# A hybrid encoder step on one core: 32 sample tokens moved from the dense expert pass to gathered rows

## The chip, the cores and the metric

The kernel runs on one core of one Trainium2 chip. The metric is the device time of one execution in microseconds (us). Three runs of the kernel before are at hand, and one profiled execution.

## What is computed

Two layers of a streaming encoder are applied to 512 prompt tokens and 32 sample tokens (544 tokens of width 1024). Each layer has a token mixer (attention, state-space scan, pooling) and then the PEER channel mixer, which takes most of the time and which the change is about. The reference, cut to that:

```python
def peer(x, w_q, sub_keys, u_tab, v_tab):          # 16384 experts, u_tab and v_tab of 16384 x 1024
    q = (xb @ w_q).reshape(blk, PEER_HEADS, 2, D_HALF)
    s = jnp.einsum('nhpd,hpkd->nhpk', q, sub_keys)
    sv, si = lax.top_k(s, PEER_TOPK)               # 16 of 128 keys, twice, for each of 8 heads
    cand = (sv[:, :, 0, :, None] + sv[:, :, 1, None, :]).reshape(blk, PEER_HEADS, 256)
    cv, ci = lax.top_k(cand, PEER_TOPK)
    ...
    eid = i1 * N_KEYS + i2                         # 128 expert slots for each token
    g = jax.nn.softmax(cv, axis=-1)
    act = jax.nn.gelu(jnp.einsum('nd,nhkd->nhk', xb, u_tab[eid]), approximate=False)
    return jnp.einsum('nhk,nhkd->nd', (g * act).astype(xb.dtype), v_tab[eid])
```

## The kernel before

The tokens lie in five tiles: tile 0 to 3 of 128 tokens, tile 4 of the 32 sample tokens. A token's 128 slots can be served in two ways, and the kernel uses both.

- **Gathered rows.** For tile 0, `gather` (lines 260 to 274) fetches with one indirect DMA on POOL's queue, for each of the 128 partitions, the row of u and v of that token's expert in one slot (1 MB). VectorE (DVE) makes the dot product with u (`junk`, line 268), ScalarE (ACT) its gelu (line 271), DVE the gate product (line 272) and the sum with v (`accg`, line 274). There are 128 such gathers in a layer, with three `uv` buffers. `gstep` paces them: each step of the dense loop has a weight (`WD1`, `WD2`), and gathers are issued in proportion.
- **Dense pass.** For the other 416 tokens (`ND`) all 16384 experts are computed, in 128 blocks of 128. `upass` (line 137) makes the 24 matmuls of a block with u (three products of high and low float32r parts over 8 pieces), each of 128x128 weights and 416 columns. `load_split` (line 125) loads 512 KB, copies the high part on ACT (line 132) and subtracts for the low part on DVE (line 133); it has three `raw` buffers. The activations are multiplied with a gate table G (expert by token), split again, and multiplied with v, 24 matmuls a block again (line 215).

A layer's PEER goes through these stages:

1. `topk` (line 285): queries, scores, and the two top-16 selections on DVE for each tile, and from them the slot tables (expert indices and gates, transposed).
2. `gbuild` (line 395) makes G in 52 steps of 8 tokens: four DVE products of 128x1024 f16 (lines 405 to 410: two comparisons, the gate's high part, the gate's low part), 16 small matmuls, two ACT evictions (line 419).
3. The spill pass (lines 170 to 174): the u pass of the first `NSPILL` = 80 blocks, whose activations go to DRAM (`AC`).
4. The dense loop (lines 182 to 232): groups of four blocks; 20 groups read their activations back from `AC`, 12 compute them with `upass`; every group makes the v pass, and the gathers run beside it.

The order of instructions on each engine is set when the kernel is built, by a scheduler that goes by the priority of the program order and by which buffers it expects to be free. On the chip each engine keeps that order, so an instruction that waits holds up those behind it. The spill pass stands behind `topk` and `gbuild` in priority, and the scheduler fills in its blocks where it sees room.

## Time and profile before

| | |
|---|---|
| median of 3 runs | 3354.44 us (3349.73 to 3357.75) |
| the profiled execution | 3355.85 us, of which the span from the first to the last instruction is 3354.1 us |
| PE (matmul) busy | 3123.9 us, 93% of the span |
| DVE busy | 2665.7 us, 79% |
| ACT busy | 1245.7 us, 37% |
| POOL busy | 644.0 us, 19% |
| mean granted TensorE clock | 0.965 |
| DMA | 781.56 MB, mean 233 GB/s |

A matmul's bar in the profile is longer than the distance to the next one, since they overlap in the array; a rate is therefore read from runs of matmuls in the chain of waits (time over count). The same holds, less strongly, for DVE and ACT: the distance between the starts of two instructions that follow each other is what one costs. "DMA share" is the mean busy share of the core's 16 DMA engines. The two layers show the same stages, the second some 1630 us after the first.

### The profile page before, as it was taken

The numbers are of one execution on the slowest core, as the hardware profiler recorded it, in microseconds if no ns is written. First come the engines' busy times: TensorE is split into PE (matmuls) and PEld (weight loads), VectorE is DVE, ScalarE is ACT, GpSimd is POOL, SyncE is SP. The second block draws the span as 40 slices with busy tenths as digits, with TensorE's granted clock in tenths as the row PEclk, the third lists the DMA queues.
The fourth block names the chain that finished last, engine by engine and source line by source line (L and its number), as shares of the span: only waits on it lengthen the run. The fifth ranks groups of instructions, "written<-read, shape, count | busy, mean of one in ns | idle before, by whom it ended". The sixth has DMA issues, their size and how long they took to land.

```text
span 3354.1 us, 48383 instructions
## 1 busy us (share of the span) xinstructions
PE 3123.9 (93%) x17932; PEld 2960.0 (88%) x17932; DVE 2665.7 (79%) x5685; ACT 1245.7 (37%) x2215; POOL 644.0 (19%) x436
## 2 busy tenths in 40 slices
PE   5779967999999999999999998789999999999998
PEld 5667967999999999999988688689999999999998
DVE  7976599993398898888974638999627989899888
ACT  3243323453333333333344423245433333333333
POOL 4443011100021222222210410120001222222221
PEclk8889988999999999999999999899999999999999
DMA  3113223677599999999952132257847999999996
GB/s 119 52 33 115 85 87 115 250 269 245 174 344 334 326 338 350 343 330 340 344 174 67 51 117 90 98 172 278 294 162 263 345 337 346 327 342 343 338 337 248
DMA packets 328265, 781.56 MB, mean 233 GB/s; under 512 B 24318, under 2 KB 178142, under 8 KB 291676
## 3 DMA queue, kind: packets, MB, share of 16 engines
q1 hardware_dynamic: 291164, 510.01, 45.1%
q0 software_dynamic: 36864, 268.45, 20.6%
q8 instruction: 141, 2.31, 0.3%
q14 instruction: 96, 0.79, 0.1%
HBM read 677.65 MB, written 100.73 MB: 232 GB/s over the span
## 4 chain that ended last, share of the span: by engine, by line
PE 48%; issue 22%; DVE 20%; DMA 7%; ACT 2%; POOL 1%; SPq 0%; POOLq 0%; ACTq 0%; DVEq 0%
PE psa L145 12%; PE psb L215 12%; PE psc L215 6%; PE psa L215 6%; DMA raw<-in_peer_uv 4%; PE psa L1012 3%; DVE ul L133 2%; DVE wl L133 1%; DMA uv<-in_peer_uv,eid 1%; DMA act<-AC 1%; DVE trep L281 1%; DVE accg L274 1%; DVE junk L268 1%; DVE X L280 1%; DVE X L283 1%
## 5 line engine op out<-in xcount | busy, mean ns | idle before, releaser
L145 PE MATMUL psa<-hh,ul 128*128 128x416 f32 (+1 forms) x2304 | 807.9, 355 | 87.7 <-DVE ul L133 87.7
L145 PE MATMUL psa<-hh,uh 128*128 128x416 f32 (+1 forms) x2304 | 805.3, 353 | 8.5 <-ACT uh L132 8.4
L145 PE MATMUL psa<-hl,uh 128*128 128x416 f32 (+1 forms) x2304 | 798.9, 350 | 0.0
L265 POOL DMA_INDIRECT uv<-in_peer_uv,eid x256 | 376.5, 1471 | 1770.5 <-DVE accg L274 1673.5
L133 DVE TENSOR_TENSOR ul<-raw,uh 128x1024 fp32r<-128x1024 f32 x268 | 345.3, 1290 | 278.4 <-ACT uh L132 278.2
L145 PEld LDWEIGHTS psa<-hh,ul 128*128 128x128 f32 x2304 | 440.1, 192 | 102.8 <-DVE ul L133 98.4
L132 ACT ACTIVATE uh<-raw 128x1024 fp32r<-128x1024 f32 x272 | 287.5, 1058 | 599.8 <-PE psa L145 510.4
L145 PEld LDWEIGHTS psa<-hh,uh 128*128 128x128 f32 x2304 | 440.7, 193 | 17.5 <-ACT uh L132 12.2
L145 PEld LDWEIGHTS psa<-hl,uh 128*128 128x128 f32 x2304 | 440.3, 193 | 6.0
L132 ACT ACTIVATE wh<-raw 128x1024 fp32r<-128x1024 f32 (+1 forms) x303 | 314.9, 1047 | 229.4 <-DMA raw<-in_peer_uv 165.3
L133 DVE TENSOR_TENSOR wl<-raw,wh 128x1024 fp32r<-128x1024 f32 (+1 forms) x281 | 342.5, 1222 | 55.3 <-ACT wh L132 54.6
L215 PE MATMUL psb<-wh 128*128 128x416 f32 x1024 | 358.1, 353 | 7.2 <-ACT wh L132 7.2
L215 PE MATMUL psb<-wh,wl 128*128 128x416 f32 x1024 | 359.4, 352 | 3.2 <-DVE wl L133 3.1
L215 PE MATMUL psb<-wl,wh 128*128 128x416 f32 x1024 | 357.9, 350 | 0.0
L274 DVE SCALAR_TENSOR_TENSOR accg<-uv,gw,accg 128x1024 f32<-128x1024 f32 x256 | 327.9, 1281 | 3.0
L268 DVE SCALAR_TENSOR_TENSOR junk<-uv,xg 128x1024 f16<-128x1024 f32 x256 | 312.0, 1219 | 21.4 <-DMA uv<-in_peer_uv,eid 21.0
L271 ACT ACTIVATE gw<-gact 128x1 f32<-128x1 f32 x256 | 50.7, 199 | 468.0 <-DVE junk L268 466.8
L196 ACT ACTIVATE wh<-act 128x416 fp32r<-128x416 f32 x256 | 139.2, 549 | 228.0 <-DVE act L194 126.6
L215 PEld LDWEIGHTS psb<-wh 128*128 128x128 f32 x1024 | 192.6, 188 | 11.1 <-ACT wh L132 9.3
L215 PEld LDWEIGHTS psb<-wh,wl 128*128 128x128 f32 x1024 | 192.5, 188 | 7.6 <-DVE wl L133 5.3
L215 PEld LDWEIGHTS psb<-wl,wh 128*128 128x128 f32 x1024 | 192.9, 188 | 1.8
L215 PE MATMUL psc<-wh 128*128 128x416 f32 x512 | 180.1, 352 | 4.9 <-ACT wh L132 4.9
(548 smaller groups left out, 5722.6 us busy)
## 6 DMA issues: line engine op xcount, KB each, us to landing
raw<-in_peer_uT SPq DMA_DIRECT2D x256, 512.0 KB, 4.4
raw<-in_peer_uv SPq DMA_DIRECT2D x256, 512.0 KB, 7.1
G<-st SPq DMA_DIRECT2D x26, 2048.0 KB, 7.3
gt<-G SPq DMA_DIRECT2D x64, 832.0 KB, 11.1
AC<-act SPq DMA_DIRECT2D x160, 208.0 KB, 2.0
act<-AC SPq DMA_DIRECT2D x160, 208.0 KB, 8.8
raw<-in_w_out SPq DMA_DIRECT2D x16, 512.0 KB, 3.3
raw<-in_peer_wq SPq DMA_DIRECT2D x16, 512.0 KB, 3.3
```

Source lines behind the costliest of these rows:

```text
L132: nc.scalar.activation(hi, raw, AF.Copy)
L133: (eng or nc.vector).tensor_sub(lo, raw, hi)
L145: nc.tensor.matmul(pss[i][:, :c - a], w[:, k, :], x[:, k, a:c], start=(k == 0 and j == 0), stop=(k == 7 and j == 2))
L196: nc.scalar.activation(wh, a_, AF.Copy)
L215: nc.tensor.matmul(ps[:, :ND], w[:, d % 4 * 128:(d % 4 + 1) * 128], x, start=(first and q == 0 and j == 0), stop=(last and q == GB - 1 and ...
L265: nc.gpsimd.indirect_dma_start(out=uv, out_offset=None, in_=s.I['peer_uv'].rearrange('l e d -> (l e) d'), in_offset=bass.IndirectOffsetOnA ...
L268: nc.vector.scalar_tensor_tensor(junk, uv[:, 0:1024], 1.0, s.xg, op0=ALU.mult, op1=ALU.mult, accum_out=act[:, i:i + 1])
L271: nc.scalar.activation(w, act, AF.Gelu)
L274: nc.vector.scalar_tensor_tensor(s.accg, rows[i][:, 1024:2048], w[:, i:i + 1], s.accg, op0=ALU.mult, op1=ALU.add)
L280: nc.vector.max_index(idx[:, 0:8], val[:, 0:8], src)
L281: nc.vector.match_replace(out=w[:n], in_to_replace=val[:, 0:8], in_values=src, imm_value=-3e38)
L1012: nc.tensor.matmul(ps[:n, :], l, ww, start=(k == 0 and i == 0), stop=(k == 7 and i == 2))
```

## The change

- Tile 4 leaves the dense pass: `ND` goes from 416 to 384. Its 32 tokens lie four times over the 128 partitions, one copy for each of four groups of slots, so that 32 more gathers serve them (`NG` 160, of which the last 32 use the inputs `xs` and the sum `accs`). At a layer's end a matmul with a selection matrix `sel` adds up the four groups.
- The spill pass has 64 blocks instead of 80, so 64 blocks are computed in the dense loop (16 groups of each kind).
- In the last 16 spill blocks (`NTAIL`) gathers are issued too, with the weight `WT` = 0.5 a block.
- The splits of the spill pass are put ahead in priority, to where `topk` begins.
- In `gbuild` (48 steps now) the product with the gate's low part goes from one DVE instruction to eight ACT instructions, each of 128x128 with the token's column of `GlT` (now float32) as its scale.

```diff
-ND = NT - D0
-NG = 128
+ND = 384
+NG = 160
-NSPILL = 80
+NSPILL = 64
+NTAIL = 16
+WT = 0.5
...
             for b in range(NSPILL):
+                with tc.high_priority(tc.cur_priority - s.early):
+                    s.pre.append(s.load_split(s.up, I['peer_uT'][layer, b], 'u'))
+                if b >= NSPILL - NTAIL:
+                    s.gate = s.lo
+                    s.gstep(WT)
                 ps, = s.upass(I['peer_uT'][layer, b])
...
+            for q in range(2):
+                ps = s.psA()
+                nc.tensor.matmul(ps[:32], s.sel, s.accs[:, q * 512:(q + 1) * 512], start=True, stop=True)
+                o = xs[1][:32, 1024 + q * 512:1536 + q * 512]
+                nc.vector.tensor_add(o, ps[:32], o)
...
-        total = NSPILL // GB * WD1 + (128 - NSPILL) // GB * WD2
+        total = NTAIL * WT + NSPILL // GB * WD1 + (128 - NSPILL) // GB * WD2
...
+        s.early = tc.cur_priority
         pend = []
         for t, (t0, n) in enumerate(TILES):
...
-            if t == 0:
-                ef = p.tile([128, 128], F32, name='ef', bufs=1)
+            if t in (0, 4):
+                a, c = (0, 128) if t == 0 else (128, 160)
...
-                nc.vector.tensor_tensor(A, A, bc(GlT), op=ALU.mult)
+                for i in range(8):
+                    a, b = i // 2, i % 2
+                    nc.scalar.activation(A[:, a, :, b], A[:, a, :, b], AF.Copy, scale=GlT[:, n0 + i:n0 + i + 1])
```

Two places show how this moves instructions. The first is ACT in the gate stage (`gbuild`), early in it. Before, `st` (an eviction of gate values) alternates with the spill pass: `uh` is the high part of a block of u and `act` the gelu of a block:

```order
L419 ACTIVATE st<-psb 128x128x4
L419 ACTIVATE st<-psc 128x128x4
L132 ACTIVATE uh<-raw 128x1024
L173 ACTIVATE act<-psa 128x416
L419 ACTIVATE st<-psb 128x128x4 x2
L419 ACTIVATE st<-psc 128x128x4
L419 ACTIVATE st<-psb 128x128x4
L132 ACTIVATE uh<-raw 128x1024
L173 ACTIVATE act<-psa 128x416
```

Now the products with the gate's low part (`A<-A,glt`) fill ACT's queue there:

```order
L435 ACTIVATE A<-A,glt 128x128 x5
L444 ACTIVATE st<-psb 128x128x4
L435 ACTIVATE A<-A,glt 128x128 x2
L444 ACTIVATE st<-psc 128x128x4
L435 ACTIVATE A<-A,glt 128x128 x7
L444 ACTIVATE st<-psb 128x128x4
```

Between the first gate product and the last eviction of layer 0, ACT has 22 pairs of `uh` and `act` before and 3 of each now, beside 384 products and 96 evictions; ahead of that stretch it has 32 pairs before and 42 now.

The second place is DVE at the end of the gate stage and in the spill pass behind it. Before, `ul` (the low part of a block of u) stands among the gate products and then 27 times in a row:

```order
L409 TENSOR_TENSOR Ah<-A,ght 128x1024
L133 TENSOR_TENSOR ul<-raw,uh 128x1024
L410 TENSOR_TENSOR A<-A,glt 128x1024
L133 TENSOR_TENSOR ul<-raw,uh 128x1024 x27
L194 TENSOR_TENSOR act<-act,gt 128x416
```

Now no `ul` stands among the last 114 gate products, and gathers (`junk`, `gw`, `accg`) stand between those that follow:

```order
L428 TENSOR_TENSOR A<-iota_83,i1t 128x1024
L430 TENSOR_TENSOR B<-iota_83,i2t 128x1024
L432 TENSOR_TENSOR Ah<-A,ght 128x1024
L138 TENSOR_TENSOR ul<-raw,uh 128x1024 x3
L288 SCALAR_TENSOR_TENSOR junk,gact<-uv,xg 128x1024
L292 TENSOR_TENSOR gw<-gw,gsl 128x1
L295 SCALAR_TENSOR_TENSOR accg<-uv,gw,accg 128x1024
L138 TENSOR_TENSOR ul<-raw,uh 128x1024
```

From the first selection to the first gate product DVE has 33 `ul` before and 44 now; 11 gathers stand ahead of the dense loop now, none before. On PE, 674 matmuls of the u pass follow the last gate matmul of layer 0 without a break before, and 552 now; in both cases 96 of them belong to the first group of the dense loop, which stands ahead of the first v matmul.

## Rows read from the trace of the kernel before

**Rows 1.** Windows by stage: us, busy PE, PEld, DVE, ACT, POOL, PEclk, DMA share, GB/s.

```profile
388.00:608.00 220.00, 173.22 (x862) 162.64 (x861) 209.60 (x966) 68.59 (x103) 33.26 (x10) 0.89 0.31 101
608.00:777.00 169.00, 168.63 (x1446) 155.09 (x1445) 156.00 (x237) 91.44 (x166) 7.80 (x4) 1.00 0.77 281
777.00:904.00 127.00, 127.00 (x674) 125.84 (x673) 38.19 (x33) 44.14 (x61) 0.00 (x0) 1.00 0.56 192
904.00:1708.00 804.00, 790.98 (x4170) 777.20 (x4169) 713.29 (x1080) 283.24 (x479) 179.85 (x126) 1.00 0.94 332
2535.00:3339.00 804.00, 792.27 (x4179) 778.88 (x4177) 713.41 (x1084) 282.99 (x477) 184.07 (x126) 1.00 0.93 330
```

**Rows 2.** Lines 405, 419 and 215: durations in ns, first and last start.

```profile
L405 DVE TENSOR_TENSOR A<-iota,i1t x104: 670/685/696, 607.9 to 2398.2; 128x1024 f16<-128x1024 f16 x104
L419 ACT ACTIVATE st<-psb x63: 583/597/629, 622.2 to 776.6; 128x512 f32<-128x512 f32 x63
L215 PE MATMUL psb<-wh x512: 344/352/458, 903.7 to 1704.0; 128*128 128x416 f32 x171
```

**Rows 3.** The chain of waits: runs of matmuls (start, us, what, count).

```profile
1633.69 18.03 PE psa L145 x96
1770.26 4.90 PE psa L1226 x39
```

**Rows 4.** Timeline of DVE: a low part, a gather's two products; two gate products.

```profile
1299.82 1.22 DVE L133 TENSOR_TENSOR ul<-raw,uh 128x1024 fp32r<-128x1024 f32 x1
1300.96 1.22 DVE L268 SCALAR_TENSOR_TENSOR junk<-uv,xg 128x1024 f16<-128x1024 f32 x1
...
1303.95 1.28 DVE L274 SCALAR_TENSOR_TENSOR accg<-uv,gw,accg 128x1024 f32<-128x1024 f32 x1
1305.16 0.58 DVE L198 TENSOR_TENSOR wl<-act,wh 128x416 fp32r<-128x416 f32 x1
```

**Rows 5.** Timeline of ACT: plain and pointer-scaled copies, evictions, a spill block.

```profile
194.50 0.69 ACT L701 ACTIVATE V<-psa 128x272 f32<-128x272 f32 x2
...
574.13 0.27 ACT L384 ACTIVATE i1t<-psc 128x128 f16<-128x128 f32 x1
574.29 0.28 ACT L385 ACTIVATE i2t<-psc 128x128 f16<-128x128 f32 x1
...
761.40 1.09 ACT L419 ACTIVATE st<-psb 128x512 f32<-128x512 f32 x2 [0.73 <-PE psb L417]
762.80 1.06 ACT L132 ACTIVATE uh<-raw 128x1024 fp32r<-128x1024 f32 x1 [0.31 <-PE psa L145]
763.76 0.50 ACT L173 ACTIVATE act<-psa 128x416 f32<-128x416 f32 x1
...
1880.47 0.86 ACT L1300 ACTIVATE hh<-psa,pc 128x272 fp32r<-128x272 f32 x2
```

**Rows 6.** Groups by form: three kinds of ACT instruction.

```profile
L333 ACT ACTIVATE e<-e 128x128 f32<-128x128 f32 x8 | 2.5, 311 | 1.1 <-DVE e L332 0.9
L1364 ACT ACTIVATE P<-psc,mx 128x128 f32<-128x128 f32 x8 | 2.8, 368 | 1.4 <-DVE mx L1359 1.4
L1300 ACT ACTIVATE hh<-psa,pc 128x272 fp32r<-128x272 f32 x8 | 3.5, 480 | 1.8 <-PE psa L1298 1.8
```

**Rows 7.** DMA queues: the dense loop (first two), the spill run 800 to 880.

```profile
q1 hardware_dynamic: 103447, 134.84, 51.2%
q0 software_dynamic: 18000, 131.08, 42.0%
...
q1 hardware_dynamic: 5062, 12.81, 46.4%
```

**Rows 8.** Windows of 100 us in the dense loop, columns as in rows 1.

```profile
940.00:1040.00 100.00, 100.00 (x524) 98.91 (x524) 90.55 (x139) 36.50 (x61) 24.51 (x17) 0.99 0.98 343
1240.00:1340.00 100.00, 97.58 (x514) 95.58 (x513) 90.05 (x138) 35.32 (x62) 24.07 (x17) 1.00 0.99 350
```

**Rows 9.** Waits, 960 to 1680 (us in total, times, longest us).

```profile
ACT wh L132 <- DMA raw<-in_peer_uv: 67.7, 34, 4.7
```

More of the change, by code (lines that the diff above doesn't have):

```diff
@@ L66, in __init__ @@
         s.xg = s.pers.tile([128, 1024], F32, name='xg')
+        s.sel = c.tile([128, 32], F32, name='sel')
         s.gain = s.pers.tile([128, 1024], F32, name='gain')
+        s.XS = s.dram.tile([32, 1024], F32, name='XS')
         s.XR = s.dram.tile([NT, 1024], F32, name='XR')
@@ L72, in consts @@
             s.nc.sync.dma_start(t, s.I[n])
+        s.nc.vector.tensor_reduce(s.sel, s.ident.rearrange('p (g n) -> p n g', g=4), axis=AX.X, op=ALU.add)
     def psA(s):
@@ L132, in load_split, with upass @@
         nc.scalar.activation(hi, raw, AF.Copy)
-        (eng or nc.vector).tensor_sub(lo, raw, hi)
+        s.lo = (eng or nc.vector).tensor_sub(lo, raw, hi).ins
         return hi, lo
-    def upass(s, src, eng=None, CH=((D0, NT),)):
+    def upass(s, src, eng=None, CH=((D0, D0 + ND),)):
         nc = s.nc
@@ L157, in peer @@
             GhT = one('ght', [128, ND], F16)
-            GlT = one('glt', [128, ND], F16)
-            s.eid = one('eid', [128, 128], I32)
-            s.gsl = one('gsl', [128, 128])
+            GlT = one('glt', [128, ND])
+            s.eid = one('eid', [128, NG], I32)
+            s.gsl = one('gsl', [128, NG])
             with ExitStack() as tk:
@@ L176, in peer @@
             s.acc = wp.tile([128, 8, ND], F32, name='acc', bufs=1)
+            s.accs = wp.tile([128, 1024], F32, name='accs', bufs=1)
+            nc.gpsimd.memset(s.accs, 0.0)
+            s.xs = wp.tile([128, 1024], F32, name='xs', bufs=1)
+            for g in range(4):
+                nc.sync.dma_start(s.xs[g * 32:(g + 1) * 32], s.XS)
             gp = dense.enter_context(tc.tile_pool(name='g', bufs=2))
@@ L226, in peer @@
                         ps = s.psA()
-                        for t, (t0, n) in enumerate(TILES[1:]):
+                        for t, (t0, n) in enumerate(TILES[1:4]):
                             nc.tensor.transpose(ps[:n, t * 128:(t + 1) * 128], s.acc[:, d, t0 - D0:t0 - D0 + n], s.ident)
-                        for t, m, n in ((1, 2, 128), (3, 1, 128), (4, 1, 32)):
+                        for t, m, n in ((1, 2, 128), (3, 1, 128)):
                             o = xs[(t - 1) // 2].rearrange('p (a b) -> p a b', a=2)[:n, (t + 1) % 2:(t + 1) % 2 + m, d * 128:(d + 1) * 128]
@@ L267, in gather @@
             with s.tc.issue_after(s.gate):
-                nc.vector.scalar_tensor_tensor(junk, uv[:, 0:1024], 1.0, s.xg, op0=ALU.mult, op1=ALU.mult, accum_out=act[:, i:i + 1])
+                nc.vector.scalar_tensor_tensor(junk, uv[:, 0:1024], 1.0, s.xg if s0 < 128 else s.xs, op0=ALU.mult, op1=ALU.mult, accum_out=act[:, i:i + 1])
             rows.append(uv)
@@ L273, in gather @@
         for i in range(KP):
-            nc.vector.scalar_tensor_tensor(s.accg, rows[i][:, 1024:2048], w[:, i:i + 1], s.accg, op0=ALU.mult, op1=ALU.add)
+            acc = s.accg if s0 < 128 else s.accs
+            nc.vector.scalar_tensor_tensor(acc, rows[i][:, 1024:2048], w[:, i:i + 1], acc, op0=ALU.mult, op1=ALU.add)
     def top16(s, pool, src, n, val, idx):
@@ L368, in topk @@
             nc.vector.tensor_add(f2, M[:, :, 0], M[:, :, 1])
-            if t == 0:
-                ef = p.tile([128, 128], F32, name='ef', bufs=1)
+            if t in (0, 4):
+                a, c = (0, 128) if t == 0 else (128, 160)
+                ef = p.tile([128, 128], F32, name='ef', bufs=1)[:, 0:c - a]
                 nc.vector.scalar_tensor_tensor(ef, f1.rearrange('p a b -> p (a b)'), 128.0, f2.rearrange('p a b -> p (a b)'), op0=ALU.mult, op1=ALU.add)
-                nc.vector.tensor_scalar(s.eid, ef, float(layer * 16384), None, op0=ALU.add)
-                nc.vector.tensor_scalar(s.gsl, e.rearrange('p a b -> p (a b)'), 1.0 / GSC, None, op0=ALU.mult)
+                nc.vector.tensor_scalar(s.eid[:, a:c], ef, float(layer * 16384), None, op0=ALU.add)
+                nc.vector.tensor_scalar(s.gsl[:, a:c], e.rearrange('p a b -> p (a b)'), 1.0 / GSC, None, op0=ALU.mult)
                 continue
             def slots(t=t, t0=t0 - D0, f1=f1, f2=f2, e=e):
-                m = 128 if t < 4 else 32
+                m = 128
                 ps = s.psV()
@@ L1016, in out_proj_ @@
         s.norm_tile(xn, xt[:n], t, 2 + layer)
+        if n == 32:
+            nc.sync.dma_start(s.XS, xn[:32])
 def mix0(s):
```

## The prediction

> **What bounds the kernel now.** The page's 40 slices come first: PE is at 9 tenths almost everywhere, so the question is where it isn't and what stands beside it. I cut each layer's PEER into four stages at the first gate product, the last gate eviction and the first v matmul [rows 2] and asked for a window of each [rows 1]. The selection stage (388 to 608) is DVE's: DVE busy 209.6 of 220 us, PE 173 at a granted clock of 0.89, its matmuls waiting for low parts that stand among DVE's selections. The gate stage (608 to 777) has PE busy throughout, since blocks of the spill pass fill it, with DVE busy 156 and ACT 91 of 169. The spill run (777 to 904) is PE alone: 674 matmuls in 127 us, DVE 38. The dense loop takes 804 us in either layer, with PE busy 791, DVE 713 and a DMA share of 0.94: three resources close to full, PE first.
>
> What a matmul costs is read from runs in the chain [rows 3]: 96 with 416 columns in 18.03 us, 187.8 ns each; 39 with 272 columns in 4.90 us, 125.6 ns. The slope is 62.2/144 = 0.43 ns a column, so 384 columns should cost 187.8 - 32 x 0.43 = 174 ns.
>
> I sum for one layer and double it, against the profiled execution's 3355.85 us (0.04% above the median 3354.44).
>
> **Selection stage: +7.** Now 44 low parts stand in it on DVE, 33 before. A low part costs 1.14 us, from its start to the next one's [rows 4]: 11 x 1.14 = +12.5. DVE's 10.4 us of idle time [rows 1] should shrink as loads and low parts come earlier; I give back half: -5. Bounds: +2 (all idle time goes) to +13 (none). PE has 42 blocks to do instead of 32; 42 x 24 x 174 ns = 175 us still fits in 227.
>
> **Gate stage: -16.** DVE loses one of its four products a step and four of 52 steps. But eight ACT products a step come in, 48 x 8 = 384, in one queue with 96 evictions. Two plain 128x128 copies start 0.16 us apart; two of 272 columns with a scale from a pointer take 0.86 us together, which with 0.48 for one puts the second 0.38 behind the first, where plain ones are 0.29 apart (0.69 less some 0.40): the pointer adds 0.09 [rows 5, 6]. That makes 0.25 us a product; the input lies in SBUF here, and a 128x128 instruction from SBUF is some 0.03 longer than a copy from PSUM (311 against 278 ns, [rows 5, 6]), of which I take half: 0.265. Evictions are 0.49 us apart (1.09 for two of 0.60), and three spill blocks cost 0.96 + 0.50 each [rows 5]. So ACT needs 384 x 0.265 + 96 x 0.485 + 3 x 1.46 = 101.8 + 46.6 + 4.4 = 153 us, in place of a stage of 169. DVE (144 products, cheaper than before) and PE no longer set it, and the spill pass no longer fills it: the order has no block among the last 114 gate products. Bounds for a product: 0.16 (no price for the pointer), 0.368 (nothing overlaps, the duration of a 128x128 instruction with a pointer, [rows 6]).
>
> Here the Trainium skill speaks against the change: its page "ScalarE: Activation LUTs", Rules for kernel authors, says to multiply on VectorE and not ScalarE, and budgets about 0.3 us plus 0.83 ns an element for an ACTIVATE with a pointer operand. By it a product is 0.41 us, and the stage would be an estimated 156 + 51 = 207 us instead of 153.
>
> **Spill run: -28.** 552 matmuls follow the last gate matmul without a break, 674 before: 552 x 174 ns = 96 us, plus 3 for a clock that has fallen while PE idles in the gate stage (the selection stage shows 0.89 at four fifths busy, [rows 1]; bounds 0 and 10): 99 instead of 127. Eleven gathers run beside it, two DVE products of 1.14 and 1.21 us each [rows 4]: 11 x 2.35 = 26 us, beside 38 that DVE had in 127 us [rows 1]. DVE has room, and the DMA share of 0.56 too. What they can cost is a low part queued behind a `junk` that waits for its row: 0 to 10 us.
>
> **Dense loop: +23.** PE: 3072 matmuls with v and 60 blocks x 24 with u (one group's four blocks stand ahead of it) are 4512 x 174 ns = 785 us; before it was 4128 x 187.8 = 775 of 804, so 29 us were transposes and waits. At the same loss: 814. DMA: the software queue's 131.08 MB are 125 gathers in 0.42 x 804 = 338 us, 2.70 us of full share each [rows 7]; 146 remain in the loop, +21 x 2.70 = +57. Sixteen more blocks of u: in the spill run 18 loads and 18 stores of activations took 0.464 x 80 = 37 us, 2.06 a pair [rows 7]; by bytes (0.52 and 0.21 MB) 1.4 for a load: +22. Sixteen fewer reads of activations at 0.65: -10. Gate tables and activations are 8% narrower, of some 154 us: -12. Sum: 756 + 57 = 813, say 812 us of full share. The share held over 100 us is at best 0.98 and 0.99, the first with PE always busy, the second with PE losing 2.4% [rows 8]; at 0.98 the loop takes 828, so 827. DVE: 21 gathers and 16 low parts add 21 x 2.6 + 16 x 1.14 = 73, the narrower products take 13 off: 773 of 827, 93% where it was 89%. So DMA bounds the loop and PE waits a little more; the stall goes from a full PE to transfers of v that come late, a wait seen already on ACT (67.7 us, [rows 9]).
>
> **Costed at nothing.** The sum over the four slot groups is two matmuls and two additions of 512 columns a layer, at most 4 x 0.6 us (an eviction's size, [rows 5]); the sample tile is the last to be normed, behind four others. Loads of `xs`, the clearing of `accs`, and the store behind it fall on POOL and SP, where POOL is busy 180 of 804 us.
>
> **Sum.** 7 - 16 - 28 + 23 = -14 us a layer, -28 in all: 3355.85 - 28 = **3328 us**.
>
> **Rivals.**
> - **The loop is bound by transfers at the share it has now** (slower). If 0.94 [rows 1] is what three `raw` buffers and three `uv` buffers sustain, since each reload waits for DVE, the loop takes 812/0.94 = 863: +59, a layer +22, 3400 us. For it: DVE, which frees the buffers, gets fuller too. Against: 0.98 with no PE loss in one stretch. It decides from a mean share of 0.964 on (841 us), where the loop eats what the other stages give.
> - **PE keeps its pace** (faster). 814 us, a share of 0.997: +10, a layer -27, 3302 us. The Trainium skill, page "DMA: Bandwidth & Descriptors", Specifications, puts HBM at about 358 GB/s for a core; the best row here is 350 over 100 us, and this case wants an estimated 356. So it is possible, hardly more.
> - **ScalarE's products don't overlap** (slower). At 0.368 a product, 0.60 an eviction and 1.56 a block the gate stage is 141 + 58 + 5 = 204, +35 instead of -16: a layer +37, 3430 us. By the skill's rule above, an estimated 207. Against: the overlap of neighbours in [rows 5].
> - **The pointer is free** (faster). At 0.16: 61 + 47 + 4 = 112, a layer -55, 3246 us.
> - **The narrower matmul saves nothing**, because loading weights sets the pace (PEld is busy 777 of 804, [rows 1]): 4512 x 187.8 ns + 29 = 876 for the loop, +72, and the run 107: a layer +43, 3442 us. Against: 272 columns run at 125.6 ns with the same weights [rows 3].
>
> **Chances.** A measurement tells about 0.2% from no change, 6.7 us: faster is below 3348, slower above 3361. Forecast 0.45 (its own range 3300 to 3355); loop at its present share 0.27; PE's pace 0.15; products not overlapping 0.05; pointer free 0.05; no gain by width 0.03. Faster: 0.37 of the forecast's 0.45, with 0.15 and 0.05: 0.57. Slower: 0.23 of the second case, 0.02 of the first, 0.08 from products that do not overlap and from no gain by width: 0.33. Same: 0.10. The range, 3285 to 3402, reaches from beyond PE's pace (selection and spill run at their low bounds) to the loop at its present share, and leaves out the last three cases and some tails, some 0.18.
>
> **What would show it.** The gate stage some 153 us long with ACT busy nearly all of it, PE under half; 552 u matmuls at 174 ns behind it; the dense loop 827 us, DMA share 0.98, DVE 93%, PE 95% busy; the first v matmul 37 us earlier after the start of the selections. I am wrong if the loop is near 860, if the gate stage is not ACT's, or if DVE waits for gathered rows in the spill run.

## The result, and the profile after

The changed kernel takes **3391.82 us** (median of 4 runs, 3387.58 to 3393.91) against 3352.09 for the kernel before in the same comparison (4 runs, 3346.8 to 3357.75): ratio 1.0118, 95% interval 1.0106 to 1.0131, slower by 1.2%. The forecast was 3328, faster. The profiled execution is 3387.58 us with a span of 3385.6, so 31.5 more than the span before, and the granted clock is 0.931 instead of 0.965.

Windows of the changed kernel by stage, with the columns of [rows 1], then 120 us from the middle of the gate stage by themselves:

```profile
394.00:614.00 220.00, 197.91 (x1076) 190.66 (x1075) 215.96 (x948) 85.03 (x124) 33.15 (x10) 0.97 0.39 133
614.00:781.00 167.00, 145.35 (x867) 91.33 (x866) 96.01 (x149) 163.92 (x490) 4.78 (x4) 0.60 0.45 180
781.00:880.00 99.00, 99.00 (x553) 99.00 (x552) 60.31 (x74) 37.87 (x63) 18.64 (x12) 0.97 0.91 322
880.00:1710.00 830.00, 798.11 (x4506) 784.58 (x4505) 763.56 (x1164) 301.93 (x525) 214.57 (x146) 1.00 0.97 348
2526.00:3356.00 830.00, 800.69 (x4505) 789.24 (x4504) 763.44 (x1160) 300.74 (x525) 220.07 (x146) 0.99 0.96 347
...
640.00:760.00 120.00, 103.97 (x586) 59.71 (x584) 70.89 (x112) 120.00 (x364) 0.00 (x0) 0.53 0.41 170
```

The edges are the first and last starts of three lines, which answer to [rows 2] (first layer):

```profile
L428 DVE TENSOR_TENSOR A<-iota,i1t x48: 683/693/694, 613.8 to 766.6; 128x1024 f16<-128x1024 f16 x48
...
L444 ACT ACTIVATE st<-psc x39: 574/786/1002, 627.4 to 781.0; 128x512 f32<-128x512 f32 x39
...
L230 PE MATMUL psb<-wh x512: 334/334/446, 879.6 to 1709.4; 128*128 128x384 f32 x171
```

The gate stage is ScalarE's from end to end: 120.00 busy of 120. TensorE's busy time is the misleading entry. Its weight loads are busy for only 59.71 of 120 us, and its clock stands at 0.53, mostly on the lower level of 1.2 GHz. A product takes part in one of two gate matmuls, and that one waits for it, so these come 0.29 us apart, a product's pace:

```profile
691.27 0.27 PE L442 MATMUL psc<-A,B 128*128 128x128 f16 x1
691.33 0.31 PE L441 MATMUL psc<-Ah,B 128*128 128x128 f16 x1
691.56 0.26 PE L442 MATMUL psc<-A,B 128*128 128x128 f16 x1
```

The same stage before kept TensorE at full clock with 1446 matmuls [rows 1]; now there are 867.

Here is where the 31.5 us are. A stage runs from first selection to first gate compare, to last eviction, to first v matmul, to last v matmul, and the end of the span. The two layers of either kernel differ by at most 2.0 us in each stage, and the table has their mean.

| us a layer | selection | gate stage | spill run | dense loop | behind the last v matmul |
|---|---|---|---|---|---|
| before | 235.8 | 168.7 | 127.1 | 804.3 | 15.5 |
| after | 244.0 | 168.0 | 98.2 | 838.7 | 21.2 |
| measured difference | +8.2 | -0.7 | -28.9 | +34.4 | +5.7 (once) |
| forecast | +7 | -16 | -28 | +23 | 0 |

The miss is 59.5 us of span: twice 15.3 in the gate stage, twice 11.4 in the loop, 5.7 at the end; selection and spill run account for less than one.

### The profile page after: what moved, and what is told of

The parts are those of the page before. It is cut to its first block, busy times and chain, and to the rows that moved or that the text cites. A ratio compares the mean times of both kernels' runs of the same rounds, so it can differ in the third digit from the quotient of the medians.

```text
span 3385.6 us, 48961 instructions
## 1 busy us (share of the span) xinstructions
PE 3111.2 (92%) x17790; PEld 2873.7 (85%) x17790; DVE 2726.4 (81%) x5800; ACT 1450.3 (43%) x3009; POOL 746.4 (22%) x502
## 4 chain that ended last, share of the span: by engine, by line
PE 42%; DVE 28%; DMA 12%; ACT 11%; issue 7%; POOL 1%; SPq 0%; POOLq 0%; DVEq 0%; ACTq 0%
PE psa L150 18%; DMA raw<-in_peer_uv 7%; PE psb L230 7%; ACT A L435 6%; DVE ul L138 4%; PE psc L230 3%; PE psa L230 3%; PE psa L1037 3%; DVE wl L138 3%; DMA uv<-in_peer_uv,eid 3%; ACT st L444 2%; DVE junk L288 2%; DVE accg L295 2%; DVE trep L302 1%; ACT wh L137 1%
## 5 line engine op out<-in xcount | busy, mean ns | idle before, releaser
L150 PE MATMUL psa<-hh,ul 128*128 128x384 f32 (+1 forms) x2304 | 770.3, 340 | 73.4 <-DVE ul L138 73.1
L150 PE MATMUL psa<-hh,uh 128*128 128x384 f32 (+1 forms) x2304 | 774.5, 340 | 2.6 <-ACT uh L137 1.2
L285 POOL DMA_INDIRECT uv<-in_peer_uv,eid x320 | 476.8, 1490 | 1342.8 <-DVE accg L295 1063.4
L150 PE MATMUL psa<-hl,uh 128*128 128x384 f32 (+1 forms) x2304 | 766.4, 336 | 0.0
L230 PE MATMUL psb<-wh 128*128 128x384 f32 x1024 | 342.8, 338 | 19.8 <-ACT wh L137 19.5
L230 PE MATMUL psb<-wh,wl 128*128 128x384 f32 x1024 | 343.3, 336 | 4.9 <-DVE wl L138 4.9
L230 PE MATMUL psb<-wl,wh 128*128 128x384 f32 x1024 | 341.8, 335 | 0.0
L291 ACT ACTIVATE gw<-gact 128x1 f32<-128x1 f32 x320 | 63.5, 198 | 550.7 <-DVE junk L288 550.4
L435 ACT ACTIVATE A<-A,glt 128x128 f16<-128x128 f16 x768 | 284.8, 616 | 0.3 <-DVE Ah L432 0.3
L211 ACT ACTIVATE wh<-act 128x384 fp32r<-128x384 f32 x256 | 132.0, 523 | 164.1 <-DVE act L209 129.9
```

The source lines that it names most:

```text
L150: nc.tensor.matmul(pss[i][:, :c - a], w[:, k, :], x[:, k, a:c], start=(k == 0 and j == 0), stop=(k == 7 and j == 2))
L211: nc.scalar.activation(wh, a_, AF.Copy)
L230: nc.tensor.matmul(ps[:, :ND], w[:, d % 4 * 128:(d % 4 + 1) * 128], x, start=(first and q == 0 and j == 0), stop=(last and q == GB - 1 and ...
L285: nc.gpsimd.indirect_dma_start(out=uv, out_offset=None, in_=s.I['peer_uv'].rearrange('l e d -> (l e) d'), in_offset=bass.IndirectOffsetOnA ...
L291: nc.scalar.activation(w, act, AF.Gelu)
L435: nc.scalar.activation(A[:, a, :, b], A[:, a, :, b], AF.Copy, scale=GlT[:, n0 + i:n0 + i + 1])
```

## The experiments

Every run is paired with the kernel before on its chip. This table has them all, with the stage means of both layers in the one profiled execution, which can lie up to 0.7% off the run's median.

| run | us (median) | ratio to before, 95% interval | selection | gate | spill run | loop | end |
|---|---|---|---|---|---|---|---|
| gate_dve | 3255.32 | 0.9707 to 0.9741 | 244.2 | 186.6 | 15.9 | 835.7 | 20.9 |
| gate_split | 3265.70 | 0.9735 to 0.9761 | 244.8 | 174.9 | 20.1 | 844.3 | 20.9 |
| before_act | 3572.35 | 1.0643 to 1.0672 | 234.0 | 181.5 | 225.7 | 804.0 | 15.5 |
| act_mix | 3355.35 | 0.9998 to 1.0030 | 244.5 | 223.0 | 19.2 | 844.3 | 21.0 |
| before_early | 3298.34 | 0.9822 to 0.9856 | 243.9 | 169.1 | 89.8 | 801.9 | 15.5 |
| rows_only | 3302.59 | 0.9845 to 0.9873 | 235.0 | 195.3 | 22.3 | 853.5 | 21.0 |
| pe_less | 3391.48 | 1.0086 to 1.0130 | 244.1 | 168.0 | 98.1 | 843.4 | 21.1 |
| dve_less | 3474.40 | 1.0316 to 1.0384 | 244.0 | 167.9 | 97.5 | 889.3 | 20.9 |
| dve_pe_less | 3403.32 | 1.0136 to 1.0187 | 244.5 | 168.0 | 98.2 | 833.2 | 20.9 |
| fewer_rows | 3371.47 | 1.0052 to 1.0078 | 244.5 | 167.9 | 97.4 | 831.9 | 18.2 |
| ring4 | 3436.74 | 1.0235 to 1.0274 | 245.1 | 167.9 | 99.3 | 860.6 | 20.9 |
| gather_end | 3393.30 | 1.0094 to 1.0133 | 244.6 | 167.9 | 97.6 | 841.8 | 21.0 |
| sum_last | 3398.26 | 1.0132 to 1.0161 | 244.3 | 167.9 | 98.3 | 842.2 | 21.3 |
| no_sum | 3390.21 | 1.0099 to 1.0135 | 244.4 | 167.9 | 97.5 | 840.0 | 20.4 |
| best68 | 3276.75 | 0.9755 to 0.9800 | 244.7 | 195.8 | 20.7 | 825.1 | 20.9 |
| best68s | 3271.78 | 0.9754 to 0.9779 | 245.3 | 197.2 | 19.7 | 827.7 | 21.0 |
| best60 | 3297.29 | 0.9823 to 0.9865 | 244.0 | 182.8 | 16.2 | 861.2 | 21.0 |
| split60 | 3266.82 | 0.9724 to 0.9754 | 244.1 | 172.0 | 15.7 | 858.9 | 21.2 |

### The products off ScalarE, all of them and half

gate_dve, against the changed kernel:

```diff
-            GlT = one('glt', [128, ND])
+            GlT = one('glt', [128, ND], F16)
...
-                for i in range(8):
-                    a, b = i // 2, i % 2
-                    nc.scalar.activation(A[:, a, :, b], A[:, a, :, b], AF.Copy, scale=GlT[:, n0 + i:n0 + i + 1])
+                nc.vector.tensor_tensor(A, A, bc(GlT), op=ALU.mult)
```

> The changed kernel with the low gate products back on DVE (one 128x1024 product a step instead of eight on ScalarE). Theory A, ScalarE's queue sets the gate stage (eight products 0.293 us apart and two evictions 0.475 apart are 3.3 us a step, 48 steps 159 us): without them DVE's four products set it, 192 x about 0.65 us (96 us busy with three) plus some 6 at the start, 130 us instead of 167; -37 us a layer, 3392 - 74 = 3318 us. Theory B, TensorE at the lower of its clocks sets it (768 matmuls at 0.167 us of its busy time, and 17 us of blocks, 145): the stage stays at 145 or more, 3348 us or above. Theory C, the time went in the dense loop and the tail alone: no change, 3392.

gate_split, where `GlH` is a float16 copy of `GlT`:

```diff
-                for i in range(8):
+                nc.vector.tensor_tensor(A[:, 0:2], A[:, 0:2], bc(GlH)[:, 0:2], op=ALU.mult)
+                for i in range(4, 8):
```

> The changed kernel with four of the eight low products of each step on DVE (one 128x512 product) and four on ScalarE. Theory A: ScalarE 4 x 0.293 + 2 x 0.475 = 2.12 us a step, 102 us; DVE 3.5 products of 0.65 us, 109 us; with 6 at the start a stage of 116 instead of 167: -51 a layer, 3290 us. Theory B (TensorE at the lower clock): at best 134 to 145, 3326 to 3348 us. Theory C: no change.

Measured: 3255.32 and 3265.70. So the rest of the change, without its ScalarE products, is 2.8% **faster** than the kernel before, and the products turn it into 1.2% slower: 137 us for one of a step's four products. For gate_dve theory A had the right sign, a size too small by 63 us and a wrong reason (for gate_split, 3290, it was too small by 24). The stage did not shrink to 130; it grew to 186.6, and the spill run behind it all but vanished. These are windows of gate_dve, gate stage and spill run:

```profile
615.00:800.00 185.00, 170.68 (x1416) 159.20 (x1414) 179.64 (x269) 94.02 (x166) 27.27 (x15) 0.94 0.87 323
800.00:816.00 16.00, 0.02 (x1) 0.00 (x0) 0.80 (x2) 0.95 (x3) 0.95 (x1) 0.63 0.80 264
```

With 1416 matmuls instead of 867 in the stage, all spill blocks are done by its last eviction. What counts is gate stage and spill run together: 202.5 us here, 195.0 in gate_split, 266.2 in the changed kernel, 295.8 before. Theory C falls with it, and B as well: at 185 us with DVE busy 179.64, TensorE's clock is 0.94. In gate_split ScalarE carries 192 products a layer without harm, since blocks still fit in between: its gate stage and spill run are 7.5 us a layer shorter than gate_dve's. Its total is no better, since its loop is 8.6 longer (844.3 against 835.7); why is not shown.

### The products alone

before_act is the kernel before with the ScalarE loop above and a float32 `GlT`, nothing else.

> The kernel before with one part of the change alone: the low gate products on ScalarE, eight a step, 52 steps. Theory A (products 0.293 us apart): ScalarE needs 52 x 3.3 = 172 us for them and 1.46 for each block of the spill pass that stays between them (25 blocks, 36 us); by the order that it takes the stage is 172 to 208 instead of 169, and what blocks leave it come later: +3 to +39 us a layer, 3358 to 3430 us. Theory B, my forecast's 0.265: 52 x 3.09 = 161 and blocks, so between -8 and +28 a layer, with a middle of +10, 3372. Theory C, ScalarE's products cost nothing by themselves: 3352.

It takes 3572.35 us, +220, beyond every theory. The stage itself came out as A had it (181.5, within 172 to 208). But only 88 matmuls of the u pass stayed in it, under four blocks, where 614 had been before, and the run behind it went from 127 to 226 us. Windows of gate stage and spill run:

```profile
605.00:787.00 182.00, 158.76 (x921) 98.75 (x920) 103.03 (x164) 178.31 (x540) 7.80 (x4) 0.57 0.42 170
787.00:1014.00 227.00, 227.00 (x1195) 224.79 (x1195) 64.47 (x55) 75.02 (x103) 0.00 (x0) 0.99 0.52 180
```

1195 matmuls stand in that run where 674 stood [rows 1]. 521 more at 187.8 ns [rows 3] are 98 us, which is the run's whole growth of 98.6. So the price of the products is mostly not the longer stage (12.8 us) but the blocks that had been hidden in it beside DVE's work. For two layers that is (12.8 + 98.6) x 2 = 223, against a loss of 220.

### The products kept, the blocks put back between them

act_mix is the changed kernel with its 384 products, written so that the blocks come in between (`spill` is the body of the loop over blocks):

```diff
+            for b in range(42):
+                spill(b)
             with ExitStack() as gs:
-                s.gbuild(gs, I1T, I2T, GhT, GlT, G)
+                s.gbuild(gs, I1T, I2T, GhT, GlT, G, spill)
...
+                if n0 % 16 == 8 and s.nb < NSPILL:
+                    spill(s.nb)
+                    s.nb += 1
```

> The changed kernel with its eight products a step left on ScalarE, but with the program written so that blocks 42 to 63 of the spill pass stand between the gate steps, one behind every second step, instead of behind all of them. Theory A, the loss is TensorE's idle time, which the order leaves unfilled: ScalarE then has 384 x 0.293 + 96 x 0.475 + about 25 blocks x 1.46 = 195 us and some 5 at the start, and no spill run is left behind it but some 10 us: gate stage and spill run 210 together instead of 266, -56 a layer, 3392 - 112 = 3280 us. Theory B, a product on ScalarE is dear in itself (a full queue in which each block's split and Gelu wait behind products): the two stages stay above 245, 3350 us or more.

3355.35 us: no difference from the kernel before, 36 less than the changed kernel, a third of what A hoped for. Windows of the stage and of what follows:

```profile
615.00:832.00 217.00, 180.54 (x1326) 153.29 (x1325) 142.04 (x215) 191.88 (x538) 35.17 (x15) 0.86 0.69 252
832.00:852.00 20.00, 18.05 (x94) 17.73 (x94) 7.02 (x9) 6.73 (x11) 0.95 (x1) 0.92 1.00 297
```

Order alone is therefore worth 24 us a layer (242.2 for the two stages together, from 266.2), and another 40 remain to gate_dve's 202.5. ScalarE is busy 191.88 of 217 us: its queue holds products, evictions, splits and Gelus, and each stands behind the others. B's threshold for the total was met, its stage bound of 245 in one layer of two (236.4 and 247.8). Both mechanisms are there, neither alone.

### The other two parts alone

before_early, against the kernel before:

```diff
             for b in range(NSPILL):
+                with tc.high_priority(tc.cur_priority - s.early):
+                    s.pre.append(s.load_split(s.up, I['peer_uT'][layer, b], 'u'))
                 ps, = s.upass(I['peer_uT'][layer, b])
```

> The kernel before with one part of the change alone: the loads and low parts of the spill pass get the priority of the selections' start (416 columns, 128 gathers, 80 spill blocks and DVE's products as before). Theory A, TensorE's 33 low parts in the selection stage become some 44: the selection stage grows by 7 us, and 11 blocks x 24 x 187.8 ns = 50 us leave the stages behind it; as DVE is full in the selection stage and in the gate stage, what is gained is TensorE's idle time there, 47 us of 220: between -20 and -43 a layer, 3270 to 3312 us. Theory B, DVE gives back in the gate stage nothing of what it spends earlier, since TensorE was full there anyway and the blocks were behind it: -5 to +7 a layer, 3342 to 3366 us.

rows_only, against gate_dve (the gathers' steps move behind `upass`):

```diff
-                with tc.high_priority(tc.cur_priority - s.early):
-                    s.pre.append(s.load_split(s.up, I['peer_uT'][layer, b], 'u'))
```

> The part of the change on the sample tokens alone: gathered rows, 384 dense columns, 64 spill blocks, gathers in the last 16 of them; the low parts are placed as in the kernel before, and the low products are DVE's. The two other parts measured so far: early low parts alone 3298 (-51), ScalarE's products alone 3572 (+220), all three 3392, without ScalarE's products 3255. Theory A, the parts are independent: 3255 + 51 = 3306 us, with the selection stage back at 236 us and a spill run of some 60 instead of 16. Theory B, the narrower matmuls gain only where early low parts keep TensorE full: 3330 us or more.

Early low parts: 3298.34, -51, within theory A; the selection stage pays 8 us and the spill run gives 37 back. Gathered rows: 3302.59, -47 against its own partner of 3349.72, where A had 3306. The stages came otherwise than I wrote (the spill run is 22.3, not 60, since DVE's products let the blocks into the gate stage; the loop is 853.5). The two parts add up: -51 and -47, and gate_dve with both is at -96 against its own partner of 3351.68.

### What bounds the dense loop

Four runs take work away from the loop, three of them from one resource each. In pe_less the v matmuls lose their third pass:

```diff
-                        for j, (w, x) in enumerate(passes(*vs[q], wh, wl)):
+                        for j, (w, x) in enumerate(passes(*vs[q], wh, wl)[:2]):
```

> The changed kernel without the third of the three partial products of each v matmul (high part of the activations with the low part of v left out): 1024 matmuls of 174 ns fewer in a loop, 178 us of TensorE's 785. All transfers, splits and DVE's work stay. Theory A, transfers or DVE (764 of 830 us) bound the loop: it stays at 815 to 835 us, 3360 to 3395 in all. Theory B, TensorE bounds it and transfers only just keep up: the loop falls below 805, the total below 3342.

dve_less loses the gather's second product, and dve_pe_less both:

```diff
-        for i in range(KP):
-            acc = s.accg if s0 < 128 else s.accs
-            nc.vector.scalar_tensor_tensor(acc, rows[i][:, 1024:2048], w[:, i:i + 1], acc, op0=ALU.mult, op1=ALU.add)
```

> The changed kernel without the second of a gather's two products (the gathered rows of v are not added up: the gathered tokens get no sum). Some 146 x 1.28 us = 187 us of DVE's 764 leave the dense loop, all transfers and TensorE's work stay, and a gather buffer comes free earlier. Theory A, transfers bound the loop: 825 to 840 us by first and last v matmul. Theory B, DVE's queue bounds it (92% busy, everything that feeds TensorE passes it in order): the loop falls to TensorE's 814 or what it does at best, and the total below 3350.

> Both cuts at once: without the second product of a gather and without the third partial product of each v matmul, so 187 us of DVE and 178 us of TensorE fewer, all transfers as they were. Theory A, transfers bound the loop: 812 to 830 us, the 812 us of full share that the forecast worked out and no less. Theory B, DVE and TensorE held it together: below 790.

fewer_rows stops a layer's gathers at 144:

```diff
-        s.gtot = min(NG, s.gtot + w * GEARLY * NG / total)
+        s.gtot = min(NG - 16, s.gtot + w * GEARLY * NG / total)
```

> The changed kernel without the last 16 of a layer's 160 gathers (half of the sample tokens' slots are left out). By the prices of the forecast 16 gathers are 43 us of full DMA share and 42 us of DVE. Theory A, transfers bound the loop: it falls from 839 to the bound that TensorE sets with its waits, 814, and the stretch behind the last v matmul stays at 21: 3392 - 50 = 3342 us. Theory B, something else does (TensorE with its held groups, or the residual's end): less than 10 us a layer, 3372 or more.

Window of the loop, first of pe_less, then of dve_less, then of dve_pe_less:

```profile
880.00:1710.00 830.00, 680.09 (x3505) 645.10 (x3503) 758.74 (x1157) 300.60 (x526) 228.88 (x146) 0.93 0.97 346
```

```profile
880.00:1710.00 830.00, 763.30 (x4205) 751.47 (x4203) 562.38 (x958) 282.02 (x492) 154.69 (x144) 0.96 0.93 333
```

```profile
880.00:1710.00 830.00, 679.71 (x3471) 649.05 (x3471) 596.57 (x1010) 303.43 (x524) 156.71 (x146) 0.92 0.96 349
```

With 178 us of TensorE's work gone the loop is 843.4 us, not one microsecond shorter, and moves 346 GB/s where it moved 348. With TensorE's and DVE's work gone it is 833.2, 3.2 above the end of theory A's range, in the fastest of four executions (the median is 22 us longer, some 11 a layer); both engines then idle a good part of the time, and the DMA share is where it was. So neither engine's amount of work bounds the loop, and transfers do for most of it. The surprise is dve_less, which neither theory had: less work on DVE made the loop 51 us **longer**, at a lower share of 0.93 (in the slowest of four executions; by the medians some 41). The waits of ScalarE for loads of v in 880 to 1710 (us in total, times, longest), in the changed kernel and in dve_less:

```profile
ACT wh L137 <- DMA raw<-in_peer_uv: 83.8, 47, 5.6
```

```profile
ACT wh L137 <- DMA raw<-in_peer_uv: 156.3, 51, 9.8
```

ScalarE waits longer for loads of v. That this comes from gather buffers that are released sooner is not shown: dve_pe_less has the same cut on DVE, its loop is about as long as the changed kernel's, and its wait is 93.0 us. The order of the instructions moved with the edits too, and what makes dve_less slower stays open.

fewer_rows falls by 6.8 us in the loop and 3.0 behind it, 20 in all, far from A's 50. Its windows tell why, the whole loop and its first 720 us:

```profile
880.00:1710.00 830.00, 800.32 (x4525) 788.74 (x4523) 729.58 (x1109) 300.19 (x512) 191.78 (x131) 0.99 0.93 330
880.00:1600.00 720.00, 691.67 (x3900) 681.37 (x3899) 658.70 (x1002) 258.68 (x450) 188.54 (x128) 0.99 0.97 348
```

The DMA share is the last column but one: 0.93 over the whole loop, 0.97 over its first 720 us. The gathers left out were the last ones, so most of the loop runs at the changed kernel's share, and only the last 110 us have room. There TensorE is full: the two rows leave it busy 108.65 of 110 us. So the loop gained less than theory B's 10 us: where TensorE is full, dropped transfers give little back.

### The gathers' buffers and the end

ring4 gives gathers a fourth buffer in the loop (`gq` is a pool of one buffer, opened there), gather_end sets GEARLY to 1.15:

```diff
-            uv = s.gp.tile([128, 2048], F32, name='uv')
+            uv = (s.gq if s.gq and s0 % 4 == 3 else s.gp).tile([128, 2048], F32, name='uv')
```

> The changed kernel with a fourth buffer for gathered rows in the dense loop (every fourth gather uses it); the constants that place the gathers are as they were. Theory A, three buffers set the gathers' pace (146 gathers in 830 us, 5.7 us each, POOL waiting 498 + 116 us for accg and accs), so that they end with the loop whatever the order says, and hold the buffers of the residual: with four they end some 20 us before the last v matmul, transposes run between v matmuls again, and each layer's loop loses 8 us, the second layer's end 5: 3392 - 21 = 3371 us. Theory B, transfers bound the loop (share 0.97): gathers in flight at four don't help, 3385 us or more. Theory C, the end is longer by its own new work (sum over slot groups): no change.

> The changed kernel with one constant altered (GEARLY 1.05 to 1.15), so that the last of the 160 gathers stand at 87% of the loop's weight instead of 95%. Theory A, the gathers that end late hold the three buffers that the residual's loads need, so that transposes, additions and stores of the end come one after the other: the stretch behind the last v matmul falls from 29 to about 15 us in the second layer, some 6 less in the first, 3392 - 20 = 3372 us; the dense loop stays within 3 us. Theory B, the longer end is the new sum over slot groups and the extra additions: under 5 us gained, 3387 or above. Theory C, the loop is held by gathers packed closer: it loses more than the end gains, above 3392.

ring4 is 45 us slower than the changed kernel, all of it in the loop (860.6), at a share of 0.96; ScalarE's wait for loads of v is 119.2 us there in the same window, against 83.8. The rival that held the share down by too few buffers falls for the gathers' three; a fourth `raw` buffer was not tried. That more gathers in flight delay the loads that TensorE needs next fits this wait, but is an inference: fewer_rows has a wait of 100.8 us in a loop that is 6.8 shorter. gather_end changed nothing: the last `accs` addition starts at 3359.7 of 3391.2, so the edit did not bring the gathers forward (3354.5 of 3385.6 in the changed kernel), and theory A was not tested by it.

In sum_last the sum over slot groups stands behind the prompt tiles, in no_sum it is left out:

```diff
-            for q in range(2):
-                ps = s.psA()
-                nc.tensor.matmul(ps[:32], s.sel, s.accs[:, q * 512:(q + 1) * 512], start=True, stop=True)
...
+                for q in range(2 if t == 4 else 0):
```

> The changed kernel with the sum over the four slot groups (two matmuls, two additions a layer) written behind the four prompt tiles' norms instead of ahead of them. Theory A, DVE takes its work in order, and the two additions and their wait for the float32 matmuls (1.85 us) stand ahead of four norms: the stretch from the last v matmul to the end falls from 21 to some 17 us in the second layer, 3392 - 4 to 3392 - 8 us in all, hardly more than a measurement can tell; the stretch itself shows it. Theory B, that stretch is set by late residual loads: 21 us as before.

> The changed kernel without the sum over slot groups (its two matmuls and two additions a layer are left out; what the gathers of the sample tokens give is not added). Theory A, the sum sets the longer end: the stretch from the last v matmul to the end falls from 21 to 16 us, 3392 - 10 = 3382 us with both layers. Theory B, the end is longer because residual loads, transposes and norms run later: 20 us or more, and no difference of the totals that can be told.

The end stays at 21.3 and 20.4 us, so the sum is not what made it longer, and costing it at nothing was right. (sum_last's total is 6 us above the changed kernel's, and its loops are 3.5 us longer each; that is not explained here.) DVE's timeline of the changed kernel there (start, us, idle time before and its releaser):

```profile
3354.51 1.27 DVE L295 SCALAR_TENSOR_TENSOR accs<-uv,gw,accs 128x1024 f32<-128x1024 f32 x1
...
3356.66 1.09 DVE L247 TENSOR_TENSOR uv<-psa,uv 128x256 f32<-128x256 f32 x3 [0.35 <-DMA uv<-XR]
3357.67 1.28 DVE L128 SCALAR_TENSOR_TENSOR raw<-uv,rs,gain 128x1024 f32<-128x1024 f32 x1
3359.60 0.69 DVE L247 TENSOR_TENSOR uv<-psa,uv 128x128 f32<-128x128 f32 x3 [0.66 <-DMA uv<-XR]
3360.95 1.90 DVE L247 TENSOR_TENSOR uv<-psa,uv 128x256 f32<-128x256 f32 x6 [0.66 <-PE psa L243]
3364.76 0.56 DVE L237 TENSOR_TENSOR acc<-psa,acc 128x384 f32<-128x384 f32 x1 [1.91 <-PE psa L230]
```

The last gather's addition starts 31 us ahead of the end of the span (29 in the kernel before), but 10 us ahead of the last v matmul at 3364.4, where it was 14 (3325.0 and 3338.6). Residual additions (L247) then wait for residual loads in the buffers that the gathers leave, for 0.35 and 0.66 us in these lines. In ring4 the last addition starts 21 us ahead of the last v matmul, and the end is 20.9 us all the same. With fewer_rows it falls to 18.2. So what makes the end 5.7 us longer is only partly the late rows, and the rest stays open.

### Where a better version lies

best68 and best60 are gate_dve with NSPILL 68 and 60; best68s adds sum_last's edit; split60 is gate_split with 60.

> The changed kernel with the low products on DVE and 68 spill blocks instead of 64. In the run with 64, TensorE idles for 16 us between the last gate eviction and the first v matmul, waiting for the gate table. Four blocks more are 96 matmuls x 174 ns = 16.7 us, which would fill just that; the loop has four blocks fewer to do (16.7 us of TensorE, some 3 of DMA, 4 low parts of DVE) and four reads of activations more. Theory A, transfers bound the loop: -3 to -6 a layer, 3243 to 3249 us. Theory B, TensorE bounds it: -14 a layer, 3227. Theory C, DVE is full until the last eviction (180 of 185 us), so the four blocks come behind it and lengthen the way to the first v matmul: 3255 or more.

> The kernel of the run before this one, with the sum over slot groups behind the four prompt tiles as well. Theory A: 4 to 8 us below the run with 68 blocks alone. Theory B: no difference.

> The low products on DVE and 60 spill blocks instead of 64. DVE is busy 180 of 185 us in the gate stage of the run with 64. Theory A, DVE sets that stage: four low parts of 1.14 us fewer, -5 a layer there, and some 3 to 5 more in the loop: 3245 to 3258 us. Theory B, TensorE sets it: -5 to -13 a layer, 3230 to 3245 us.

> The low products half on DVE and half on ScalarE, and 60 spill blocks instead of 64. In the run with 64 the gate stage and what follows to the first v matmul take 195 us with TensorE busy 171, DVE 168 and ScalarE 150 of 185. Theory A, TensorE sets that stage and transfers the loop: 16.7 us of TensorE leave the first and cost the second some 3 of DMA and little else: -5 to -13 a layer, 3240 to 3256 us. Theory B, TensorE's work is worth as much in the loop: 3260 to 3270.

None is better than gate_dve, whose 3255.32 us (0.9707 to 0.9741 of before) beat both kernels; split60 cannot be told from gate_split. Four blocks more lengthen gate stage and spill run by 14 us and shorten the loop by 11 (best68, in a profiled execution of 3261.1 us of span, among its faster ones of 3257.68 to 3283.82), as theory C had it; best68s adds no difference that the intervals tell. Four fewer cost the loop 25 us (best60, 3297.29, above both of its theories) and 15 (split60), where some 3 to 5 were expected. In split60 about half of the 15 is the executions: its profiled one is the slowest of five and gate_split's the fastest, and its median of 3266.82 lies where theory B put it. So a block of the u pass costs the loop more than its transfers by my prices, although TensorE's time alone costs it nothing (pe_less). Which of its steps does that isn't settled.

## Why the prediction was wrong

- **Selection stage, +7**: +8.2. Right, and TensorE does its blocks in it, 197.91 busy of 220 at a clock of 0.97.
- **Gate stage, -16: this step failed.** That ScalarE sets the stage, that DVE and TensorE do not, that no block fills it, was forecast and is what the windows show. The size of the term was wrong, and mostly by this: a product priced at 0.265 us. ScalarE's timeline in the changed kernel gives it, four products between two evictions:

```profile
690.04 1.47 ACT L435 ACTIVATE A<-A,glt 128x128 f16<-128x128 f16 x4
691.21 0.74 ACT L444 ACTIVATE st<-psb 128x512 f32<-128x512 f32 x1
691.69 0.89 ACT L435 ACTIVATE A<-A,glt 128x128 f16<-128x128 f16 x2
692.27 0.75 ACT L444 ACTIVATE st<-psc 128x512 f32<-128x512 f32 x1
```

  From 690.04 to 691.21 are four starts, 0.293 us a product; two in 691.69 to 692.27 give 0.29. An eviction is 0.48 (691.21 to 691.69; forecast 0.485). Then 384 x 0.293 + 96 x 0.48 + 4.4 = 163 us, where the window has 163.92 busy; the first product starts 5.7 us behind the first compare (619.5 and 613.8). That makes 168 where 153 was forecast, and leaves no gain: 11 us by the products, and 6 by the start, which the sum did not have. I had taken 0.09 for the pointer and 0.16 for the rest, from two plain copies that read PSUM, with half of a difference of 0.03 for SBUF; together these fall short by 0.028, and the whole of that difference would have left 0.01. No run separates the two parts. The bounds of 0.16 and 0.368 held.
  The Trainium skill has the price, on the page "ScalarE: Activation LUTs", in the section "What ACT_TABLE_LOAD costs": 186 ns with immediate operands, 0.833 ns an element, some 93 ns for each pointer operand, and an overlap of some 93 ns between neighbours. By it a product is an estimated 186 + 107 + 93 - 93 = 293 ns, and the trace agrees. By the page, then, the pointer's 0.09 was right, and the plain part is 0.20 and not 0.16; no run here shows a plain one of 128 columns that reads SBUF. By the same figures `uh` in [rows 5], which does at 1024 columns, is an estimated 186 + 853 - 93 = 946 ns, and the trace has 0.96 us, so that row would have been nearer than the copies that read PSUM. The figure that the prediction cited from the same page's Rules for kernel authors (0.41 us) leaves the overlap out, and the stage of 207 us that it gave was not seen. That rule's advice, to multiply on VectorE, held: 3255 against 3392.
- **Spill run, -28**: -28.9. 552 matmuls in 98.2 us (553 in the window of 99), with the gathers beside them at no visible cost. Right, and misleading: gate_dve shows that with the products elsewhere there is no run left to shorten. I took the emptied gate stage as given, priced the two stages one after the other, and never asked what the same blocks would cost if they had stayed in the gate stage. The sum for the run was right and that for the stage too low by 15; but the choice to compare the change only with the kernel before, as one piece, hid that two of its parts are worth -51 and -47 and the third +137.
- **Dense loop, +23**: +34.4. The volume was right: 153.10 MB for 146 gathers in 0.477 of 830 us, 2.71 us each (2.70 forecast), as the queues in 880 to 1710 show, the gathers' queue last:

```profile
q1 hardware_dynamic: 99068, 135.33, 48.9%
q0 software_dynamic: 21024, 153.10, 47.7%
```

  With the other queues that is 0.97 of 830, 805 us of full share against 812. What failed is the share at which the loop holds: I took 0.98, a row of 100 us [rows 8], for the mean; it is 0.97 and 0.96, and 805 us at 0.98 would have been 821. That is the rival with transfers at the present share, in a mild form, and the runs without some of the engines' work show that it is not TensorE's amount of work. What keeps the share at 0.97 (buffers, order, or the transfers themselves) stays open. Another 4 us a layer lie in the last group: the last v matmul starts 9 us after the last one of `psb` (1718.6 and 1709.4), 5 in the kernel before (1709.0 and 1704.0).
- **Costed at nothing**: the sum over slot groups was (no_sum is within the interval of the changed kernel). The residual's loads were not in the list at all. The end is 5.7 us longer, of which late rows explain some 3 (fewer_rows).
- **What was to show it**: stage of 153 with ScalarE busy throughout (167, busy), TensorE under half (not so: its weight loads are busy 91 of 167 us, its matmuls 145), 174 ns a matmul (right), loop of 827 at 0.98 and DVE 93% (839, 0.97, 92%), first v matmul 37 us earlier after the start of the selections (21).

The range held the time partly by luck: its room on the slow side was meant for the loop, and half of the miss came from the gate stage. The sign was wrong because 28 us were forecast as the sum of terms of up to 56 (both layers), of which the gate stage alone was off by 31 and the loop by 23.

## What to carry to other kernels

Before moving work to an idle engine, look for what the present bound hides: the kernel before hid a third of a TensorE pass in the gate stage beside DVE (614 of the spill pass's 1920 matmuls), and the move took that shadow away, for 98 us a layer in the plain case (before_act). Price stages that share a filler together, and each part of a change by itself, since two good parts can carry a bad one. Where transfers hold a loop, freeing an engine or adding a buffer can cost time, as dve_less and ring4 did, and a run of its own has to tell.

## What was not expected of the hardware

- TensorE at its lower level while it looks busy: in 640 to 760 its busy time is 103.97 of 120 us at a granted clock of 0.53; over the whole stage it is granted 0.60, and 0.94 with blocks between the gate matmuls (gate_dve).
- 187 us less work on DVE made a loop bound by transfers 51 us longer, and a fourth gather buffer 22 us longer. In both, ScalarE waits longer for loads of v (156.3 and 119.2 us against 83.8); the cause is not shown.
- The loop's transfers reached 364 GB/s over 100 us (dve_pe_less, 880 to 980, share 0.99), more than the best row before, 350 [rows 8]. The Trainium skill's page "DMA: Bandwidth & Descriptors", Specifications, puts the limit of HBM for a core at about 358 GB/s, a stack's 716 GB/s over two cores; this stretch, of a kernel on one core, is 2% above it.
